# The second MLP product of a hybrid decoder step in wider matmuls, with 64 tokens as the stationary side

## The chip, the core and the metric

The kernel runs on one core of a Trainium2 chip. The metric is the time of one execution on the device, in microseconds (us). Five engines work side by side, each through its own queue of instructions in a fixed order: TensorE (PE, matmuls, with its weight loads in rows of their own, PEld), VectorE (DVE), ScalarE (ACT), GpSimd (POOL) and SyncE (SP), whose queue issues the DMA transfers. They wait for each other by semaphores.

## The reference

One step of one decoder layer for 288 tokens: 256 of a prompt, then 8 x 4 of samples. All is float32.

```python
h2 = rmsnorm(x, norm2_g)
f = jnp.square(jax.nn.relu(jnp.einsum("btd,df->btf", h2, w_ff1)))
x = x + jnp.einsum("btf,fd->btd", f, w_ff2)
```

D is 2048 and the MLP's inner width F is 8192. Before the MLP stand an input projection (2048 x 3072), a causal convolution of 31 taps, windowed means with small products, a LayerNorm and an output projection (2048 x 2048); behind it a last RMSNorm. The states of convolution and pooling are outputs too. The change is about the third line, `f` times `w_ff2`.

## The kernel before

Activations lie channel-major: 128 channels on the partitions, 288 tokens along the row. Every float32 operand of a large product is split exactly into two float32r parts, hi and lo, and a product is three: hi weight by hi activation, hi by lo, and lo by hi, summed in float32 in PSUM. In `gemm` (L223 to L236) that is three matmuls per tile of 128 x 128 weights, on lines L233, L234 and L235, each with the weights as the stationary side and 288 token columns moving.

Weights come in blocks of 1 MB, 1024 rows by 2 x 128 columns, by one DMA each (`load`, L142 to L151, queue SP), into `wr`, three buffers. `split` (L202 to L220) makes the hi part on ScalarE (L213, a cast) and the lo part on VectorE (L214, raw minus hi; in the first third also on GpSimd), 1024 columns an instruction, into four buffers each of `whi` and `wlo`. `weight_groups` is a generator of such splits in the order of use, and each `gemm` asks it for the next group at its end (`ready`), so that one group's weights are split while the group before is multiplied.

The MLP runs in four chunks of 2048 of the inner width (`FCH`), L440 to L475. In a chunk the first product makes 16 tiles of `f`, two at a time: eight `gemm` of 16 k tiles into two PSUM banks, then relu times the norm's factor (L452, DVE), the square and its hi part (L454, L456, ACT) and the lo part (L457, DVE). The second product then has eight groups of 256 output columns, each 16 k tiles by two banks by three matmuls, 96 in all, and adds the two banks to the residual `xT` (L466, DVE). Accumulators come from the pool `acc`, four banks, two for each group: the next group begins in two banks while DVE reads the other two. In the last chunk the squares for the last norm are taken on the way (L472, ACT; L474, DVE) and `xT` is scaled (L475, ACT); in the very last group one bank is finished ahead of the other (`m_outer`). `rsqrt_rows` (L177 to L197) then sums over the partitions with matmuls of one column (L182), goes through a chain of small operations, spreads the result (L196), and L481 multiplies and stores the output in six pieces.

Nobody writes the order on each engine out by hand: a scheduler with a timeline of its own orders the instructions by priority and estimated readiness, and places the waits. Thus a change of one part can shift the order of others.

Of the kernel before, what the change touches and what calls it, by code (L numbers as in the profile page):

```python
# [9 lines left out]
F32 = mybir.dt.float32  # L10
F32R = mybir.dt.float32r
# [5 lines left out]
P = 128  # L17
# [4 lines left out]
TB = T // 3  # L22
DC = DP = 1024
# [17 lines left out]
# groups of two 128-column results of the input projection, in order: a convolution tile's pair  # L41
# (a_i, gate_i), or a pooling group, the widest windows first
# [29 lines left out]
# per-channel vectors, [P, columns]: channel = column * P + partition  # L72
# [10 lines left out]
def trunk_kernel(ctx: ExitStack, tc: tile.TileContext, io):  # L83
    """Activations are channel-major: [channel on the partitions, token]. Tokens: the prompt's
    256, then 8 x 4 of the samples. Every float32 operand of a large product is split exactly in
    two float32r parts (12 bits each): w x = wh xh + wh xl + wl xh, in float32 accumulation."""
# [6 lines left out]
    actp = ctx.enter_context(tc.tile_pool(name="actp", bufs=40))  # L93
    tmpp = ctx.enter_context(tc.tile_pool(name="tmpp", bufs=8))
    prdp = ctx.enter_context(tc.tile_pool(name="prdp", bufs=2))
    acc = ctx.enter_context(tc.tile_pool(name="acc", bufs=4, space=PSUM))
    cvp = ctx.enter_context(tc.tile_pool(name="cvp", bufs=2, space=PSUM))
    msp = ctx.enter_context(tc.tile_pool(name="msp", bufs=2, space=PSUM))

# [16 lines left out]
    def act(name, **kw):  # L116
        return actp.tile([P, T], F32R, name=nm(name), **(kw or {"tag": "act"}))
# [7 lines left out]
    def f32(t):  # L125
        return t[:].bitcast(F32)
# [5 lines left out]
    vec = const.tile([P, NV], F32, name="vec")  # L132
    xT = const.tile([P, KT, T], F32, name="xT")
    u_all = const.tile([P, N8, UL], F32, name="u_all")
    z_all = const.tile([P, N8, ZL], F32, name="z_all")
# [6 lines left out]
    def load(cuts=((0, 8),), x_cuts=()):  # L142
        """The next 1 MB of weights; at the start in pieces, with pieces of x between them"""
# [18 lines left out]
    def load_table(func, src):  # L162
        """The function's table is loaded once src is there."""
# [6 lines left out]
    ident = const.tile([TB, TB], F32, name="ident")  # L170
# [6 lines left out]
    def rsqrt_rows(parts, scale, after=None):  # L177
        """PSUM [P, T], on every partition: 1 / sqrt(scale * sum over parts and partitions + eps)."""
# [14 lines left out]
        for j in range(3):  # L193
            nc.vector.tensor_scalar(dg[:TB, j * TB : (j + 1) * TB], ident, s[2][:, j : j + 1], None, op0=ALU.mult)
# [5 lines left out]
    turn = {"n": 0}  # L200

    def split(raw, share=0, cut=4):  # L202
        """[P, 8, 256] -> get(k, m): the parts of 128 columns; `share` of 8 on GpSimd"""
# [38 lines left out]
    hx = []  # L242
    for k in range(KT):
        hh, hl = act("hh"), act("hl")
# [6 lines left out]
    def weight_groups():  # L251
        """Per group of products, get(k, m) for each block of 8 k, in the order of the products."""
# [11 lines left out]
        for _ in range(2 * DFF // 256):  # L264
            yield [split(load()) for _ in range(2)]
# [23 lines left out]
    cs = []  # L289
    sum_c = row("sum_c")  # L290

    def conv_pair(i):
# [16 lines left out]
        c = actp.tile([P, T], F32, name=nm("c"), tag="c", bufs=8)  # L309
# [20 lines left out]
    dd = {}  # L330

    def pool_group(g):
# [3 lines left out]
        for m in range(2):  # L336
# [3 lines left out]
            tz = tmp("tz", T, "tz", 2)  # L340
# [4 lines left out]
            while w < WINDOWS[g]:  # L345
                s2 = tmp("s", ZL, "s", 4)
# [13 lines left out]
            dh, dl = act("dh", tag="p", bufs=16), act("dl", tag="p", bufs=16)  # L360
# [11 lines left out]
    mixp = {}  # L372
    for g in GROUPS:
        bk = bank2()
        gemm(bk, [dd[2 * g], dd[2 * g + 1]])
        for m in range(2):
            i = 2 * g + m
            mh, ml = act("ph"), act("pl")
# [21 lines left out]
    for i in range(N8):  # L400
        n = tmp("n")
        nc.vector.tensor_tensor(n, cs[i], rl[:, :T], op=ALU.mult)
        mh, ml = act("mh"), act("ml")
# [14 lines left out]
    x1 = []  # L418
    ss2 = row("ss2")
    for g in range(8):  # L420
        bk = bank2()
        gemm(bk, mixc)
        for m in range(2):
# [3 lines left out]
            kw = {"tag": "p", "bufs": 16} if k < 8 else {"tag": "c", "bufs": 8} if k >= 12 else {}  # L427
            ah, al = act("ah", **kw), act("al", **kw)
# [12 lines left out]
    r2 = row("r2")  # L441
    ssf = row("ssf")
    for ch in range(DFF // FCH):
        fx = []
        for g in range(FCH // 256):
# [4 lines left out]
            for m in range(2):  # L450
# [4 lines left out]
                fh, fl = act("fh"), act("fl")  # L455
# [85 lines left out]
```

## Time and profile before

| | |
|---|---|
| time, median of 3 runs (lowest to highest) | 1127.89 us (1125.96 to 1129.59) |
| the profiled execution, span from first to last instruction | 1125.9 us |
| PE busy | 1094.4 us, 97% |
| DVE, ACT, POOL busy | 677.1, 468.7, 188.8 us |
| mean granted TensorE clock | 0.987 |
| read from HBM | 181.49 MB, 165 GB/s over the span |
| a chunk's second product, PE | some 101 us, 768 matmuls |

No time is listed for the profiled execution beside its span; the lowest of the runs, 1125.96 us, equals the span, so that nothing that could be measured lies around it.

How to read the lines. A group of instructions reads: source line, engine, operation, tile written <- tiles read, shapes, count | busy us, mean ns of one | idle time of the engine just before, and what ended it. Names of buffers stand without their numbers: `ac` is a PSUM bank, `fh` and `fl` are the two parts of an `f` tile, `ah` and `al` those of the MLP's input, `ph` and `pl` those of the pooling half. The record of a matmul lasts longer than its slot, since matmuls are pipelined: what one costs is the distance from its start to the start of the next. A row of waits reads: who, at which line <- for whom: us in total, how often, the longest. A row of the timeline begins with its start and duration in us. A row of windows reads: from:to, length, then busy us and instructions of PE, PEld, DVE, ACT and POOL, the granted clock (1.00 is full), the share of the DMA engines and GB/s.

### The profile page before, as it was taken

How to read it: one execution, taken by the hardware profiler on the slowest of the kernel's cores; microseconds unless marked ns; L12 is line 12 of the kernel's file. 1: busy time of each engine (PE TensorE's matmuls, PEld its weight loads, DVE VectorE, ACT ScalarE, POOL GpSimd, SP SyncE). 2: the span in 40 equal slices, each digit the busy share in tenths (PEclk: the TensorE clock that was granted, in tenths of full speed). 3: DMA queues.
4: the chain of work that ended last, by engine and by line, in shares of the span. 5: the costliest groups of instructions: out<-in, count | busy, mean ns of one | idle time of the engine just before them, and what ended most of it. 6: DMA issues, size and time to landing. Idle time of an engine off the chain costs nothing.

```text
span 1125.9 us, 19336 instructions
## 1 busy us (share of the span) xinstructions
PE 1094.4 (97%) x8190; PEld 1089.8 (97%) x8190; DVE 677.1 (60%) x983; ACT 468.7 (42%) x643; POOL 188.8 (17%) x149
## 2 busy tenths in 40 slices
PE   7998898999999999999999999999999999999995
PEld 7998898999999999999999999999999999999995
DVE  7999999788755544445555444455444445555554
ACT  6443345356544433334444333344433334444441
POOL 4789886612200000000000000000000000000000
PEclk9999998989999999999999999999999999999998
DMA  8554438534445444444445454444444454545432
GB/s 298 191 175 164 148 115 222 184 113 166 172 150 177 160 171 167 158 179 154 184 153 183 152 182 156 174 163 167 170 160 178 153 184 151 183 155 175 162 113 84
DMA packets 31910, 187.01 MB, mean 166 GB/s; under 512 B 3408, under 2 KB 7760, under 8 KB 10448
## 3 DMA queue, kind: packets, MB, share of 16 engines
q1 hardware_dynamic: 31824, 185.78, 47.0%
q8 instruction: 64, 1.05, 0.4%
q14 instruction: 22, 0.18, 0.0%
HBM read 181.49 MB, written 4.28 MB: 165 GB/s over the span
## 4 chain that ended last, share of the span: by engine, by line
PE 86%; DVE 9%; POOL 2%; issue 2%; DMA 1%; ACT 0%; SPq 0%; DVEq 0%; POOLq 0%
PE ac L233 29%; PE ac L234 28%; PE ac L235 28%; DVE pc L316 3%; DVE wlo L214 1%; POOL wlo L214 1%; DVE d L354 1%; DVE ssc L397 1%; DVE d L351 1%; DMA xT<-in_xT 1%; POOL s L347 0%; DVE d L359 0%; DVE z_all L283 0%; PE pt L182 0%; DVE xT L481 0%
## 5 line engine op out<-in xcount | busy, mean ns | idle before, releaser
L213 ACT CAST whi<-wr 128x1024 fp32r<-128x1024 f32 (+1 forms) x342 | 355.0, 1040 | 562.8 <-PE ac L234 543.6
L214 DVE TENSOR_TENSOR wlo<-wr,whi 128x1024 fp32r<-128x1024 f32 (+1 forms) x295 | 364.7, 1236 | 371.8 <-ACT whi L213 371.7
L233 PE MATMUL ac<-ah,whi 128*128 128x288 f32 x1024 | 302.7, 296 | 0.0
L233 PE MATMUL ac<-fh,whi 128*128 128x288 f32 x1024 | 302.4, 295 | 0.0
L234 PE MATMUL ac<-al,whi 128*128 128x288 f32 x1024 | 301.2, 294 | 0.0
L234 PE MATMUL ac<-fl,whi 128*128 128x288 f32 x1024 | 301.2, 294 | 0.0
L235 PE MATMUL ac<-fh,wlo 128*128 128x288 f32 x1024 | 299.3, 292 | 0.0
L235 PE MATMUL ac<-ah,wlo 128*128 128x288 f32 x1024 | 298.8, 292 | 0.0
L235 PEld LDWEIGHTS ac<-fh,wlo 128*128 128x128 f32 x1024 | 193.1, 189 | 0.0
L235 PEld LDWEIGHTS ac<-ah,wlo 128*128 128x128 f32 x1024 | 192.9, 188 | 0.0
L234 PEld LDWEIGHTS ac<-fl,whi 128*128 128x128 f32 x1024 | 192.7, 188 | 0.0
L234 PEld LDWEIGHTS ac<-al,whi 128*128 128x128 f32 x1024 | 192.4, 188 | 0.1
L233 PEld LDWEIGHTS ac<-ah,whi 128*128 128x128 f32 x1024 | 192.1, 188 | 0.1
L233 PEld LDWEIGHTS ac<-fh,whi 128*128 128x128 f32 x1024 | 192.0, 188 | 0.0
L233 PE MATMUL ac<-hh,whi 128*128 128x288 f32 x384 | 113.6, 301 | 7.7 <-DVE tg L302 6.6
L214 POOL TENSOR_TENSOR wlo<-wr,whi 128x1024 fp32r<-128x1024 f32 (+1 forms) x47 | 112.3, 2400 | 34.0 <-ACT whi L213 31.4
L234 PE MATMUL ac<-hl,whi 128*128 128x288 f32 x384 | 114.9, 301 | 3.0 <-DVE hl L246 2.9
L235 PE MATMUL ac<-hh,wlo 128*128 128x288 f32 x384 | 114.2, 301 | 1.5 <-DVE wlo L214 1.4
L316 DVE SCALAR_TENSOR_TENSOR pc<-u_all,vec,pc 128x256 f32<-128x256 f32 x232 | 100.1, 479 | 1.3
L233 PEld LDWEIGHTS ac<-hh,whi 128*128 128x128 f32 x384 | 73.3, 193 | 8.4 <-issue 7.0
L234 PEld LDWEIGHTS ac<-hl,whi 128*128 128x128 f32 x384 | 74.3, 194 | 4.1 <-DVE hl L246 4.1
L235 PEld LDWEIGHTS ac<-hh,wlo 128*128 128x128 f32 x384 | 74.1, 194 | 2.3 <-DVE wlo L214 2.2
(115 smaller groups left out, 875.5 us busy)
## 6 DMA issues: line engine op xcount, KB each, us to landing
wr<-in_w SPq DMA_DIRECT2D x167, 1024.0 KB, 4.9
xT<-in_xT SPq DMA_DIRECT2D x8, 288.0 KB, 5.7
wr<-in_w SPq DMA_DIRECT2D x8, 256.0 KB, 5.6
out_u_out<-u_all SPq DMA_DIRECT2D x1, 1208.0 KB, 8.6
out_yT<-xT SPq DMA_DIRECT2D x2, 576.0 KB, 2.9
u_all<-in_hist_c SPq DMA_DIRECT2D x8, 136.0 KB, 5.8
out_z_out<-z_all SPq DMA_DIRECT2D x1, 668.0 KB, 7.4
z_all<-in_hist_p SPq DMA_DIRECT2D x4, 152.0 KB, 4.0
```

The costliest lines, as they stand in the source:

```text
L213: nc.scalar.copy(hi[:, k : k + cut, :], src)
L214: eng.tensor_tensor(lo[:, k : k + cut, :], src, hi[:, k : k + cut, :].bitcast(F32), op=ALU.subtract)
L233: nc.tensor.matmul(b, wh, xh, start=k == 0, stop=False)
L234: nc.tensor.matmul(b, wh, xl, start=False, stop=False)
L235: nc.tensor.matmul(b, wl, xh, start=False, stop=k == n - 1)
L316: nc.vector.scalar_tensor_tensor(out=dst, in0=up[:, w : w + SEQ], scalar=cwv[:, w : w + 1], in1=pc, op0=ALU.mult, op1=ALU.add)
L351: nc.vector.scalar_tensor_tensor(out=d[:, w - 1 : SEQ], in0=s[:, PH + w - 1 : ZO], scalar=1.0 / w, in1=z[:, PH + w - 1 : ZO], op0=ALU.mult ...
L354: nc.vector.scalar_tensor_tensor(out=samples(d[:, SEQ:T], NS), in0=ss[:, :, PH:], scalar=1.0 / w, in1=zs[:, :, PH:], op0=ALU.mult, op1=ALU ...
L397: nc.vector.tensor_tensor(ssc, ssc, q, op=ALU.add)
```

## The change

The second product is written anew; the first keeps its form. The tokens are divided: `TM` = 224, the main ones, and `TA` = 64, the tail. A tile of `f` now lies in one row of 576 columns: lo of the main tokens (224), hi of all (288), lo of the tail (64). So 448 adjoining columns are lo and hi of the main tokens, the 288 in the middle are hi of all, and the last 128 are hi and lo of the tail. VectorE writes the lo part in two pieces.

Output columns are taken 512 at a time, in four groups a chunk, and a group is four calls of `gemm4`, each over four k tiles (a quarter of the chunk's width). For each k tile a call issues:

- one matmul with the tail's 128 columns (hi and lo of 64 tokens) as the stationary side and 512 columns of hi weights moving, into the bank `tok`: token-major partial results, hi by hi in the upper 64 partitions, hi by lo in the lower;
- for each of four tiles of 128 output columns, one matmul of hi weights by the 448 columns, into columns 0 to 447 of that tile's bank, and one of lo weights by the 288 columns, into columns 224 to 511. So a bank holds the main tokens in two pieces that are still to be added, and the lo-weight part of the tail behind them.

All four banks of `acc` thus belong to one group, and `tok` takes a bank of the pool that the convolution used (`cvp`, two banks). `split4` splits half the rows of two blocks at once, into `vhi` and `vlo`, two buffers each of 4 x 512 columns, and the blocks of `w_ff2` come in pairs of adjoining columns. At a group's end `tok` is copied (first chunk, ACT) or added (DVE) to `y_tok` [128, 2048], and each bank is added to `xT` in two operations, of 224 and of 288 columns. In the last chunk each group's part of `y_tok` is transposed by PE against the identity (`tp`), and DVE adds its two halves to the tail's columns of `xT` before the banks' second pieces. `m_outer` is not used by the new form.

To make room, tiles that only the first part needs (`u_all`, `z_all`, `prd`, and the temporaries `tz` and `s`) are in a pool `earp` that is closed before the MLP; `latep`, which holds `y_tok`, `vhi` and `vlo`, comes in its place. Pairs of hi and lo activations are now one tile of two rows (`act`), half as many buffers of twice the size, and the convolution's results lie in pairs (`cp`).

```diff
-        for c in range(0, D, 256):
+        for c in range(0, D, 512):
             for r in range(ch, ch + FCH, 1024):
-                yield "w_ff2", r, (c, c + P)
+                for cc in (c, c + 256):
+                    yield "w_ff2", r, (cc, cc + P)
...
+    def split4(raws, h):
+        hi = late_pool[0].tile([P, 4, 512], F32R, name=nm("vhi"), tag="vhi", bufs=2)
+        lo = late_pool[0].tile([P, 4, 512], F32R, name=nm("vlo"), tag="vlo", bufs=2)
+        for j, raw in enumerate(raws):
+            src = raw[:, 4 * h : 4 * h + 4, :]
+            cols = slice(256 * j, 256 * j + 256)
+            nc.scalar.copy(hi[:, :, cols], src)
+            nc.vector.tensor_tensor(lo[:, :, cols], src, hi[:, :, cols].bitcast(F32), op=ALU.subtract)
+        return hi, lo
+
+    def gemm4(banks, tokens, rhs, first, last):
+        hi, lo = ready.pop()
+        for k, x in enumerate(rhs):
+            nc.tensor.matmul(tokens, x[:, TM + T - TA : 2 * T], hi[:, k, :], start=first and k == 0, stop=last and k == 3)
+        for m, b in enumerate(banks):
+            for k, x in enumerate(rhs):
+                cols = slice(m * P, (m + 1) * P)
+                nc.tensor.matmul(b[:, 0 : 2 * TM], hi[:, k, cols], x[:, 0 : 2 * TM], start=first and k == 0, stop=False, skip_group_check=True)
+                nc.tensor.matmul(b[:, TM:512], lo[:, k, cols], x[:, TM:512], start=False, stop=last and k == 3, skip_group_check=True)
+        ready.extend(itertools.islice(weights, 1))
...
+            for _ in range(D // 512 * FCH // 1024):
+                raws = [load(), load()]
+                for h in range(2):
+                    yield split4(raws, h)
...
-                nc.vector.tensor_tensor(fl, f, f32(fh), op=ALU.subtract)
+                nc.vector.tensor_tensor(x[:, 0:TM], f[:, 0:TM], f32(fh[:, 0:TM]), op=ALU.subtract)
+                nc.vector.tensor_tensor(x[:, TM + T :], f[:, TM:T], f32(fh[:, TM:T]), op=ALU.subtract)
...
-        for g in range(8):
-            bk = bank2()
-            gemm(bk, fx, m_outer=last and g == 7)
-            for m in range(2):
-                k = 2 * g + m
+        for g in range(D // 512):
+            tok = cvp.tile([P, 512], F32, name=nm("tok"), tag="cv")
+            bk = bank2() + bank2()
+            for j in range(FCH // 512):
+                gemm4(bk, tok, fx[4 * j : 4 * j + 4], j == 0, j == FCH // 512 - 1)
+            yt = y_tok[:, g * 512 : (g + 1) * 512]
+            if ch == 0:
+                nc.scalar.copy(yt, tok)
+            else:
+                nc.vector.tensor_tensor(yt, yt, tok, op=ALU.add)
+            if last:
+                tp = ms("tp")
+                for m in range(4):
+                    nc.tensor.transpose(tp[:, m * P : (m + 1) * P], yt[:, m * P : (m + 1) * P], ident)
+                xa = xT[:, 4 * g : 4 * g + 4, TM:T]
+                for h in range(2):
+                    nc.vector.tensor_tensor(xa, xa, tp[:].rearrange("p (m t) -> p m t", t=P)[:, :, h * TA : (h + 1) * TA], op=ALU.add)
+            for m in range(4):
+                k = 4 * g + m
                 xk = xT[:, k, :]
-                nc.vector.tensor_tensor(xk, xk, bk[m][:, :T], op=ALU.add)
+                nc.vector.tensor_tensor(xk[:, 0:TM], xk[:, 0:TM], bk[m][:, 0:TM], op=ALU.add)
+                nc.vector.tensor_tensor(xk, xk, bk[m][:, TM : TM + T], op=ALU.add)
```

More of the change, by code (lines that the diff above doesn't have):

```diff
@@ L22 @@
 TB = T // 3
+TA = 64
+TM = T - TA
 DC = DP = 1024
@@ L98, in trunk_kernel @@
     msp = ctx.enter_context(tc.tile_pool(name="msp", bufs=2, space=PSUM))
+    early = ExitStack()
+    earp = early.enter_context(tc.tile_pool(name="earp", bufs=1))
+    prdp = early.enter_context(tc.tile_pool(name="prdp", bufs=2))
     seen = {}
@@ L116, in act @@
     def act(name, **kw):
-        return actp.tile([P, T], F32R, name=nm(name), **(kw or {"tag": "act"}))
+        t = actp.tile([P, 2, T], F32R, name=nm(name), **(kw or {"tag": "act"}))
+        return t[:, 0, :], t[:, 1, :]
     def tmp(name, n=T, tag="tmp", bufs=6):
@@ L263, in weight_groups @@
             yield [split(load())]
-        for _ in range(2 * DFF // 256):
-            yield [split(load()) for _ in range(2)]
+        for _ in range(DFF // FCH):
+            for _ in range(FCH // 256):
+                yield [split(load()) for _ in range(2)]
+            for _ in range(D // 512 * FCH // 1024):
+                raws = [load(), load()]
+                for h in range(2):
+                    yield split4(raws, h)
     weights = weight_groups()
@@ L289, in trunk_kernel @@
     cs = []
+    cp = [actp.tile([P, 2, T], F32, name=nm("c"), tag="c", bufs=4) for _ in range(N8 // 2)]
     sum_c = row("sum_c")
@@ L438, in trunk_kernel @@
                     nc.gpsimd.tensor_tensor(ss2, ss2, q2, op=ALU.add)
+    early.close()
+    latep = ctx.enter_context(tc.tile_pool(name="latep", bufs=1, reuse_waits="tile"))
+    late_pool.append(latep)
     r2 = row("r2")
     ssf = row("ssf")
+    y_tok = latep.tile([P, D], F32, name="y_tok")
     for ch in range(DFF // FCH):
```

37 lines of the change are left out of this document (19 added, 18 removed).

## The prediction, made before the changed kernel had run

> **What bounds the kernel now.** I read the page's shares first, then the waits of the MLP, then its groups and the timeline.
>
> ```profile
> PE 1094.4 (97%) x8190; PEld 1089.8 (97%) x8190; DVE 677.1 (60%) x983; ACT 468.7 (42%) x643; POOL 188.8 (17%) x149
> PE 86%; DVE 9%; POOL 2%; issue 2%; DMA 1%; ACT 0%; SPq 0%; DVEq 0%; POOLq 0%
> ```
>
> TensorE holds 86% of the chain that ended last. The waits between 330 and 1111 us, where the MLP runs, have no row in which PE waits:
>
> ```profile
> ACT whi L213 <- PE ac L234: 463.5, 244, 2.1
> DVE wlo L214 <- ACT whi L213: 355.6, 245, 2.0
> DVE xT L466 <- PE ac L235: 21.5, 32, 3.2
> SPq L150 <- DVE wlo L214: 708.7, 120, 5.9
> ```
>
> Everybody waits for the matmuls, and the weight loads wait for a raw buffer. So the second product costs what its matmuls cost, and a change of it pays or loses on PE's pitch and wherever it gives PE a wait. The windows of two second products, the last and the one before it, and the ends of the last:
>
> ```profile
> 808.20:909.50 101.30, 101.30 (x770) 101.30 (x769) 46.72 (x51) 34.95 (x36) 0.00 (x0) 1.00 0.47 166
> 1010.40:1111.40 101.00, 101.00 (x771) 101.00 (x770) 49.23 (x62) 43.47 (x63) 0.00 (x0) 1.00 0.36 126
> L233 PE MATMUL ac<-fh,whi 128*128 128x288 f32 x1024 | 302.4, 295 | 0.0
> L234 PE MATMUL ac<-fl,whi 128*128 128x288 f32 x1024 | 301.2, 294 | 0.0
> L235 PE MATMUL ac<-fh,wlo 128*128 128x288 f32 x1024 | 299.3, 292 | 0.0
> 1010.51 0.29 PE L233 MATMUL ac<-fh,whi 128*128 128x288 f32 x1
> 1111.29 0.29 PE L235 MATMUL ac<-fh,wlo 128*128 128x288 f32 x1
> ```
>
> Three lines with 1024 matmuls each over four chunks make 768 per chunk: 100.78 us over 767 steps is a pitch of 131.4 ns. What would the columns alone take? At half clock the same matmul shows it:
>
> ```profile
> 239.00:242.00 3.00, 3.00 (x14) 3.00 (x14) 1.34 (x2) 1.24 (x2) 0.00 (x0) 0.50 0.70 292
> 239.17 0.44 PE L234 MATMUL ac<-pl,whi 128*128 128x288 f32 x1
> 239.41 0.44 PE L235 MATMUL ac<-ph,wlo 128*128 128x288 f32 x1
> ```
>
> 240 ns per 288 columns at a granted 0.50; halved, 120 ns, 0.4167 ns a column. So 11.4 ns of each pitch at full clock is not columns, if all of the 240 is. (With one and the same toll in both it would be 2 x 131.4 - 240 = 22.8 ns.) Only this part can the change win.
>
> **The change, part by part.**
>
> *Columns and instructions.* Per k tile and 512 weight columns the old form has 4 x 3 matmuls of 288 columns, 3456 columns. The new one has one of 512 (token stationary), four of 448 and four of 288: again 3456. No column is saved; nine matmuls stand where twelve stood, 256 times over (64 k tiles, four groups of 512).
>
> What becomes of the 11.4 ns is the unknown. If it is a toll per matmul, three tolls go: 256 x 3 x 11.4 ns = 8.7 us gained. If it is a rate (288 columns in 131.4 ns, the operands not coming faster), 512 + 4 x 448 columns cost eight old matmuls, and the gain is 0. The third reading comes from the nearest longer matmul, the float32 one of the mean:
>
> ```profile
> 222.26 0.65 PE L385 MATMUL pmean<-sum_c,ones 128*128 128x288 f32 x2
> 222.53 0.51 PE L235 MATMUL ac<-ph,wlo 128*128 128x288 f32 x1
> 222.88 0.29 PE L233 MATMUL ac<-ph,whi 128*128 128x288 f32 x1
> ```
>
> 222.26 to 222.88 less one pitch of 0.131 leaves 489 ns for two passes, 244.5 each. If each streams 240 ns, only 4.4 ns is toll: a longer pass hides it. Then wide ones cost 191.1 and 217.7 ns, the 288s stay at 131.4: 1507.7 instead of 1576.8 ns, 256 x 69.1 = 17.7 us gained (the toll of 22.8 would make 17.5). Against that stands the load alone:
>
> ```profile
> 314.59 0.25 PEld L182 LDWEIGHTS pt<-ones,ss 128*96 128x96 f32 x2
> 314.76 0.25 PEld L182 LDWEIGHTS pt<-ones,q 128*96 128x96 f32 x2
> 315.27 0.19 PEld L233 LDWEIGHTS ac<-ah,whi 128*128 128x128 f32 x1
> 315.38 0.19 PEld L234 LDWEIGHTS ac<-al,whi 128*128 128x128 f32 x1
> ```
>
> One load of 96 columns every 85 ns, one of 128 in 110: less than 120, so the load is hidden already at 288 columns and should not be what makes 131.4. I take the toll, 8.7 us, between the ends 0 and 17.7. A quarter (four k tiles) is then 6.17 us: tokens 0.90, each bank 1.32.
>
> The Trainium skill, "TensorE: Matmul & The Clock Gate", section "Back-to-back issue gap", gives columns/2.4 + 2.5 ns at full clock. For 288 that is 122.5, and the trace has 131.4: they differ. Taken for the wide matmuls alone it makes 189.2 and 215.8 ns and a gain of 20.1 us, so it speaks for the third reading.
>
> *Waits added.* Durations that the boundaries need:
>
> ```profile
> L214 DVE TENSOR_TENSOR wlo<-wr,whi 128x1024 fp32r<-128x1024 f32 x289 | 359.3, 1243 | 371.1 <-ACT whi L213 371.1
> L466 DVE TENSOR_TENSOR xT<-xT,ac 128x288 f32<-128x288 f32 x64 | 27.2, 454 | 26.4 <-PE ac L235 26.4
> L481 DVE TENSOR_TENSOR xT<-xT,pr 128x1152 f32<-128x1152 f32 x2 | 2.6, 1348 | 0.0
> L481 DVE TENSOR_TENSOR xT<-xT,pr 128x576 f32<-128x576 f32 x2 | 1.5, 746 | 0.0
> L213 ACT CAST whi<-wr 128x1024 fp32r<-128x1024 f32 x334 | 350.1, 1050 | 561.8 <-PE ac L234 543.6 <-issue 8.1 <-ACT ah L429 4.1
> L472 ACT ACTIVATE q<-xT 128x288 f32<-128x288 f32 x15 | 5.9, 434 | 9.6 <-DVE xT L466 9.6
> L475 ACT ACTIVATE xT<-xT,vec 128x288 f32<-128x288 f32 x16 | 7.7, 524 | 0.1
> DMA to landing us min/median/max: 4.5/4.9/11.1
> 1111.42 0.25 PE L182 MATMUL pt<-ones,ssf 128*96 128x1 f32 x2
> 1111.62 0.46 DVE L466 TENSOR_TENSOR xT<-xT,ac 128x288 f32<-128x288 f32 x1 [4.88 <-PE ac L235]
> 1112.60 0.33 PE L182 MATMUL pt<-ones,q 128*96 128x1 f32 x2 [0.93 <-ACT q L472]
> ```
>
> The L481 rows give 1.04 ns a column: an add of 224 columns 0.39, of 256 0.42, of 512 0.69 us. DVE sees PE's end 0.2 us late (last matmul over at 1111.42, add at 1111.62). All four accumulators now belong to one group; before, two of four were free at each change. Times below run from the start of a group's last quarter, PE's end 6.17; DVE works in the order in which the changed program issues.
>
> Between groups in chunks 1 to 3: token add 1.10-1.79, two lo splits to 4.27, then two adds of 224 and two of 288. Bank 0 is free at about 5.5 and wanted at 6.17 + 0.90: no wait. The splits' second block is loaded only when a buffer is read out 3.7 us before this quarter; 4.9 later it lands at 1.2, its copy ends at 2.3, in time. Cost 0, with 1.5 us to spare; without that cover each us of lateness costs a us.
>
> Between chunks 2 and 3, and 3 and 4, the first product starts with no token matmuls ahead, and DVE has split (3.55), token add (4.25), split (5.5), 224, 224 (6.3), 288 (6.73) before bank 0 is free: 0.6 us each, 1.2 in all. After chunk 1 ScalarE copies the tokens, and the wait is gone.
>
> In the last chunk PE transposes the tokens at each group's end: four float32 matmuls, two passes of 128 columns each at the load's 110 ns, 0.9 us, to 7.05. DVE then has two adds of 256 (to 8.1), a lo split (9.3) and the 288 add that frees bank 0 at 9.8. PE fills in with the tokens of the next two quarters (the second from 8.5, when ScalarE's two copies after 6.37 are done, to 9.4): 1.0 us idle. 1.9 us for each of three changes, 5.7.
>
> The tail: from 7.05 + 0.2 two adds of 256 and four of 288 end at 9.9. ScalarE takes squares and scales in turn (434 and 524 ns) and ends the last square at 11.4, 5.3 us after PE's last product matmul; before it was 1111.42 to 1112.60, 1.2. Cost 4.1. What follows is the same.
>
> *Hidden edits.* The lo activation written in two pieces and the split adds cost a fixed 0.155 us a piece (454 ns less 288 x 1.04), 0.3 us per 256 columns of the first product, on a DVE that is 49% busy in the last window above; nothing on the path unless DVE fills up. Loads: the same megabytes in another order, one per 6.17 instead of 6.3 us, at a DMA share of 0.47. Pooled early tiles reshuffle the instructions of the first 300 us; from nothing in the trace can I tell the sign, and take 0 within 2 us.
>
> Sum: -8.7 + 1.2 + 5.7 + 4.1 = +2.3 us. The profiled execution spans 1125.9 us, as the fastest run (1125.96); the median of the three runs is 2.0 above. 1127.9 + 2.3 = 1130.2 us.
>
> **The rivals.**
> *Wide matmuls hide the toll* (other side, faster): 17.7 instead of 8.7 gained, 1121.2 us; by the skill's formula 1118.8. For it the mean's 4.4 ns, against it the load's 110 ns. It decides from a pitch of the 448s under about 194 ns.
> *A rate, no gain* (the change does not do what it says): 448 columns cost 204 ns, 1138.9 us. For it: no toll shows at half clock or in the half-rate float32 pass, as a limit on columns per ns would have it.
> *The pairs starve* (slower): a block's load can start only when the pair before is split, three buffers serve pairs of two, and copies need all 512 columns before the first token matmul. Landing later by the 1.5 us to spare costs; with 1 us on each of 32 pairs, 1162 us. Against it the median of 4.9; for it the maximum of 11.1. A lost clock belongs here too:
>
> ```profile
> 235.32 0.33 PE L182 MATMUL pt<-ones,ssc 128*96 128x1 f32 x2 [2.04 <-DVE ssc L397]
> ```
>
> PE idled 2.04 us there, and the half clock of the window from 239 follows. The last chunk's stalls could do the same: three times 3 us at half clock lose (240 - 131) / 240 each, 4 us in all, 1134.
>
> **How the numbers follow.** Toll per matmul 0.45 (1130; alone 1125 to 1136), rate 0.20, wide hides 0.22, starving or clock 0.13. About 0.3%, 3.4 us, can be told from no change, so 1124.5 to 1131.3 is the same. Faster 0.25: the hiding case nearly whole, and the low edge of the first. Same 0.26: half of the first. Slower 0.49: its upper part and the two others. The range 1119 to 1142 leaves out the worst stalls and the best hiding.
>
> **What would show it.** Pitch: the 448s start-to-next 198 ns (hides 191, rate 204), the 512s 225 (218, 234). Waits of PE: for the DVE add before bank 0 in three places of the last chunk, about 1 us each, and little elsewhere; the chain's end with a square 5.3 us after the last product matmul. Wrong I would be by PE rows that wait for a hi copy or a load throughout the MLP, by a granted clock under 1.00 there, or by a first product that starts some us off the 301.62 of this row:
>
> ```profile
> 301.62 0.30 PE L233 MATMUL ac<-ah,whi 128*128 128x288 f32 x1
> ```

## The result, and the profile after

The changed kernel takes 1136.16 us (median of four runs, 1135.38 to 1137.22); the kernel before, on the same chip, 1126.93 us (1125.07 to 1129.59). The ratio is 1.0084, with a 95% interval from 1.0067 to 1.0101: some 9.5 us slower. 1130.2 us was predicted, in a range of 1119 to 1142; the sign was the likeliest one, the size was 6 us short (7 in the change, since a fourth run has moved the median before from 1127.89 to 1126.93). The profiled execution took 1136.49 us with a span of 1134.7, against a span of 1125.9 before: 8.8 us to be explained. Each run of the changed kernel takes 1.7 to 1.8 us more than its span. So 1125.9 will be the span of a run of some 1127.7 us, an estimate, and that the fastest run equals it does not show that nothing lies around the span, as the section on the time before has it; the forecast, added to the median, does not depend on this.

From the page of the changed kernel, the shares of the engines and the chain that ended last:

```profile
PE 1096.3 (97%) x7438; PEld 1064.0 (94%) x7438; DVE 700.9 (62%) x1131; ACT 464.9 (41%) x647; POOL 187.2 (16%) x149
PE 87%; DVE 10%; ACT 1%; issue 1%; DMA 0%; SPq 0%; DVEq 0%; POOL 0%; POOLq 0%; ACTq 0%
```

TensorE is still what counts. With 752 matmuls fewer PE is busy 1.9 us longer in all, so even there next to nothing was gained. Its waits from 300 to 1136 us, in the changed kernel:

```profile
PE pt L190 <- DVE ssf L536: 4.1, 1, 4.1
PE pr L204 <- DVE dg L202: 2.0, 1, 2.0
PE tok L249 <- ACT vhi L239: 1.7, 3, 0.6
```

The first and the last row are new; both lie in the last chunk and behind it. To see where the 8.8 us are, cut both traces at the starts of the MLP's stretches. Windows of the changed kernel: first product of chunk 2, second product of chunk 2, first product of chunk 4, second product of chunk 4 up to its last product matmul's end, the wait behind it, the norm's small matmuls, and the output:

```profile
505.21:606.78 101.57, 101.57 (x770) 101.57 (x769) 52.16 (x78) 42.73 (x60) 0.00 (x0) 1.00 0.50 175
606.78:707.06 100.28, 100.28 (x579) 93.90 (x577) 51.95 (x71) 33.67 (x36) 0.00 (x0) 1.00 0.43 158
909.02:1010.67 101.65, 101.65 (x769) 101.65 (x769) 52.82 (x80) 42.51 (x60) 0.00 (x0) 1.00 0.50 176
1010.67:1115.13 104.46, 102.71 (x591) 94.76 (x589) 53.91 (x82) 39.36 (x56) 0.00 (x0) 1.00 0.31 111
1115.13:1119.86 4.73, 0.60 (x7) 0.39 (x5) 4.06 (x10) 2.70 (x8) 0.00 (x0) 0.87 0.00 0
1119.86:1125.20 5.34, 3.32 (x14) 2.46 (x14) 1.43 (x8) 0.68 (x3) 0.00 (x0) 0.50 0.00 0
1125.20:1134.70 9.50, 0.02 (x1) 0.00 (x0) 5.28 (x6) 0.00 (x0) 0.00 (x0) 0.50 0.63 248
```

The same stretches of the kernel before (first product of chunk 2, second product of chunk 2, second product of chunk 4, the norm, the output):

```profile
505.55:606.46 100.91, 100.91 (x771) 100.91 (x769) 51.24 (x63) 42.94 (x60) 0.00 (x0) 1.00 0.47 167
606.46:707.37 100.91, 100.91 (x771) 100.91 (x770) 46.75 (x51) 34.94 (x36) 0.00 (x0) 1.00 0.47 167
1010.51:1111.42 100.91, 100.91 (x770) 100.91 (x769) 49.12 (x62) 43.47 (x63) 0.00 (x0) 1.00 0.36 126
1111.42:1116.29 4.87, 2.01 (x16) 1.38 (x14) 1.88 (x9) 1.18 (x3) 0.00 (x0) 0.99 0.00 0
1116.29:1125.90 9.61, 0.00 (x0) 0.00 (x0) 5.28 (x6) 0.00 (x0) 0.00 (x0) 0.50 0.62 246
```

All stretches, from one start to the next, in us (the middle ones read from the trace in the same way):

| stretch | before | after | difference |
|---|---|---|---|
| up to the MLP's first matmul | 301.62 | 301.80 | +0.2 |
| first products, chunks 1 to 4 | 102.60, 100.91, 100.91, 100.91 | 103.14, 101.57, 101.54, 101.65 | +2.6 |
| second products, chunks 1 to 3 | 101.33, 100.91, 101.33 | 100.27, 100.27, 100.42 | -2.6 |
| second product, chunk 4, to the last product matmul's end | 100.91 | 104.46 | +3.5 |
| from there to the end | 14.48 | 19.57 | +5.1 |

So the rewritten stretches of chunks 1 to 3 gain 2.6 us, the first products, whose code is the same but for the storage of hi and lo, lose it again, and the last chunk and its tail make the result.

Why so little is gained: the beginning of a second product in the changed kernel (timeline: start, length, instruction).

```profile
606.78 1.09 PE L249 MATMUL tok<-vhi,fx 128*128 128x512 f32 x4
607.71 0.37 PE L253 MATMUL ac<-fx,vhi 128*128 128x448 f32 x1
...
612.72 0.36 PE L253 MATMUL ac<-fx,vhi 128*128 128x448 f32 x1
612.92 0.29 PE L254 MATMUL ac<-fx,vlo 128*128 128x288 f32 x1
613.06 1.09 PE L249 MATMUL tok<-vhi,fx 128*128 128x512 f32 x4
```

607.71 less 606.78 is 0.93 us for four token matmuls, 232 ns each (225 predicted). From 607.71 to 613.06 stand 16 pairs of a 448 and a 288, 334 ns a pair, of which the 448 has some 201 (198 predicted) and the 288 some 133 (131.4). Over the 16 quarters of the chunk a quarter is 100.27 / 16 = 6.267 us; predicted were 6.17, and four k tiles of the old form at 131.4 ns took 100.91 / 16 = 6.307. Over 64 quarters that is 2.6 us gained of 8.7. (That the table has 2.6 for three chunks as well is chance: there 0.8 comes from the two stretches of 101.33.)

The change of group in the last chunk, and the tail, in the changed kernel's timeline:

```profile
1035.76 0.60 PE L520 MATMUL tp<-ident,y_tok 128*128 128x128 f32 x4
1036.11 1.18 PE L249 MATMUL tok<-vhi,fx 128*128 128x512 f32 x4
1037.87 1.20 PE L249 MATMUL tok<-vhi,fx 128*128 128x512 f32 x4 [0.58 <-ACT vhi L239]
1038.91 0.44 PE L253 MATMUL ac<-fx,vhi 128*128 128x448 f32 x1
...
1115.00 0.29 PE L254 MATMUL ac<-fx,vlo 128*128 128x288 f32 x1
1115.13 0.60 PE L520 MATMUL tp<-ident,y_tok 128*128 128x128 f32 x4
1115.33 0.39 DVE L527 TENSOR_TENSOR xT<-xT,ac 128x224 f32<-128x224 f32 x1 [0.95 <-PE ac L254]
1115.77 0.88 DVE L523 TENSOR_TENSOR xT<-xT,tp 128x256 f32<-128x256 f32 x2
1116.67 1.54 DVE L528 TENSOR_TENSOR xT<-xT,ac 128x288 f32<-128x288 f32 x4
1119.86 0.45 PE L190 MATMUL pt<-ones,ssf 128*96 128x1 f32 x2 [4.13 <-DVE ssf L536]
1120.17 0.46 PE L190 MATMUL pt<-ones,q 128*96 128x1 f32 x2
```

The four transposes take 0.35 us, the tokens of two quarters stand in a row because the banks are not free yet, and the second of them waits for ScalarE's copy. At the end DVE adds the transposed halves and four second pieces in a chain; the column sums of the square follow 5.0 us after the last product matmul's end (1115.13 to 1120.17), where it was 1.2. In that pause the granted clock falls to 0.50, as the windows show, and from these column sums to the end it is 14.5 us (1120.17 to 1134.7) where it was 13.3 (1112.60 to 1125.9).

### The profile page after: what moved, and what is told of

Same layout as the page of the kernel before. It is cut to its first block, busy times and chain, and to the rows that moved or that the text cites. A ratio compares the mean times of both kernels' runs of the same rounds, so it can differ in the third digit from the quotient of the medians.

```text
span 1134.7 us, 17926 instructions
## 1 busy us (share of the span) xinstructions
PE 1096.3 (97%) x7438; PEld 1064.0 (94%) x7438; DVE 700.9 (62%) x1131; ACT 464.9 (41%) x647; POOL 187.2 (16%) x149
## 4 chain that ended last, share of the span: by engine, by line
PE 87%; DVE 10%; ACT 1%; issue 1%; DMA 0%; SPq 0%; DVEq 0%; POOL 0%; POOLq 0%; ACTq 0%
PE ac L253 18%; PE ac L267 17%; PE ac L269 17%; PE ac L268 17%; PE ac L254 12%; PE tok L249 5%; DVE pc L356 3%; DVE d L394 1%; DVE wlo L223 1%; DVE ssc L437 1%; DVE hx L280 1%; ACT vhi L239 1%; DVE d L391 1%; DMA xT<-in_xT 0%; PE pt L190 0%
## 5 line engine op out<-in xcount | busy, mean ns | idle before, releaser
L253 PE MATMUL ac<-fx,vhi 128*128 128x448 f32 x1024 | 343.1, 363 | 0.0
L223 DVE TENSOR_TENSOR wlo<-wr,whi 128x1024 fp32r<-128x1024 f32 (+1 forms) x167 | 204.6, 1227 | 176.5 <-ACT whi L222 176.5
L267 PE MATMUL ac<-ax,whi 128*128 128x288 f32 x1024 | 302.6, 296 | 0.0
L268 PE MATMUL ac<-ax,whi 128*128 128x288 f32 x1024 | 301.1, 294 | 0.0
L269 PE MATMUL ac<-ax,wlo 128*128 128x288 f32 x1024 | 300.7, 294 | 0.0
L254 PE MATMUL ac<-fx,vlo 128*128 128x288 f32 x1024 | 299.4, 294 | 0.0
L253 PEld LDWEIGHTS ac<-fx,vhi 128*128 128x128 f32 x1024 | 191.9, 188 | 16.7 <-issue 0.8
L254 PEld LDWEIGHTS ac<-fx,vlo 128*128 128x128 f32 x1024 | 192.3, 188 | 2.5
L268 PEld LDWEIGHTS ac<-ax,whi 128*128 128x128 f32 x1024 | 193.5, 189 | 0.1
L269 PEld LDWEIGHTS ac<-ax,wlo 128*128 128x128 f32 x1024 | 193.3, 189 | 0.0
L267 PEld LDWEIGHTS ac<-ax,whi 128*128 128x128 f32 x1024 | 191.8, 187 | 0.3 <-PE ac L253 0.3
L267 PE MATMUL ac<-hx,whi 128*128 128x288 f32 x384 | 116.2, 304 | 8.5 <-DVE tg L342 6.6
L268 PE MATMUL ac<-hx,whi 128*128 128x288 f32 x384 | 115.6, 302 | 0.2
```

The lines of the kernel that those rows point to most:

```text
L223: eng.tensor_tensor(lo[:, k : k + cut, :], src, hi[:, k : k + cut, :].bitcast(F32), op=ALU.subtract)
L253: nc.tensor.matmul(b[:, 0 : 2 * TM], hi[:, k, cols], x[:, 0 : 2 * TM], start=first and k == 0, stop=False, skip_group_check=True)
L254: nc.tensor.matmul(b[:, TM:512], lo[:, k, cols], x[:, TM:512], start=False, stop=last and k == 3, skip_group_check=True)
L267: nc.tensor.matmul(b, wh, xh, start=k == 0, stop=False)
L268: nc.tensor.matmul(b, wh, xl, start=False, stop=False)
L269: nc.tensor.matmul(b, wl, xh, start=False, stop=k == n - 1)
```

## The experiments

All but e10 were run once, so each is read from the stretches of its trace, not from its time. Theory after the result: a matmul in float32r pays a toll, but wide ones pay more of it than 288 columns do; the first products are slowed by the places of hi and lo in one tile; and the last chunk pays for the transposes' adds on DVE. Rivals: a rate in columns per ns, a load of weights that is not hidden, a wait in the first products, a falling clock.

**e1: the pitch by width.** The changed kernel with blocks of 40 matmuls appended behind its end, each with other weights than the one before:

```diff
+        for name, n in (("ra", 64), ("rb", 128), ("rc", 192), ("rd", 256), ("re", 288), ("rf", 352), ("rg", 448), ("rh", 512)):
+            block(name, (n,))
+        block("oa", (288,), off=16)
+        block("ob", (448,), off=64)
+        block("la", (288,), m=64)
+        block("lb", (288,), m=32)
+        block("lc", (448,), m=64)
+        block("pp", (448, 288))
+        for name, n in (("ba", 128), ("bb", 288), ("bc", 448), ("bd", 512)):
+            block(name, (n,), s=sb, x=mb)
```

> The changed kernel, with blocks of 40 matmuls behind its last store that nothing reads (time as a whole is longer and says nothing): float32r, weights changing with each matmul, 64, 128, 192, 256, 288, 352, 448 and 512 columns, then 288 and 448 columns from other offsets, then stationary sides of 64 and 32 columns, a block that alternates 448 and 288, and bfloat16 with 128, 288, 448 and 512. Toll per matmul: the pitch is columns/2.4 + 11 to 13 ns from 256 columns up (448: 199, 512: 226), whatever the stationary side. Rate: the part over columns/2.4 grows with the columns, 11.4 ns at 288, 17.7 at 448, 20.3 at 512. Contention with the weight load: the part over columns/2.4 falls to a half or less with 64 stationary columns and to a quarter with 32 (288: 126 and 123). Wide matmuls hide it: 448 at 191, 512 at 218. If it is the 4-byte operands, bfloat16 shows 2 to 5 ns in place of 11.

Its timeline (one row is a whole block; `lc` has 64 columns of weights, `bc` and `bd` are bfloat16):

```profile
1165.56 5.43 PE L495 MATMUL re<-mv,stw 128*128 128x288 f32 x40
1170.83 6.56 PE L495 MATMUL rf<-mv,stw 128*128 128x352 f32 x40
1177.23 8.27 PE L495 MATMUL rg<-mv,stw 128*128 128x448 f32 x40
1185.33 9.25 PE L495 MATMUL rh<-mv,stw 128*128 128x512 f32 x40
1218.25 8.26 PE L495 MATMUL lc<-mv,stw 128*64 128x448 f32 x40
1240.24 7.73 PE L495 MATMUL bc<-mb,sb 128*128 128x448 bf16 x40
1247.81 8.80 PE L495 MATMUL bd<-mb,sb 128*128 128x512 bf16 x40
```

A block's length less one matmul's own record, by 39, is its pitch: 8.27 less 0.365 gives 202.7 ns for `rg`. All of them, from the starts at full clock, in ns:

| columns | 64, 192 | 256 | 288 | 352 | 448 | 512 |
|---|---|---|---|---|---|---|
| float32r | 112 | 120.4 | 131.8 | 160.0 | 202.7 | 227.3 |
| above columns x 0.4167 | | 13.7 | 11.8 | 13.3 | 16.0 | 14.0 |
| bfloat16 | | | 122.5 | | 189.2 | 215.8 |

The block of 128 columns, and that of 192 but for its last 15 steps, ran at half clock, at 213 ns a matmul. The excess is about the same for 256 and for 512 columns, so it is no rate; it does not vanish in wide matmuls, so nothing is hidden. With 64 columns of weights instead of 128 the 448 takes 202.4 and the 288 takes 130.1, so it isn't the weight load either. But the 448s and 512s pay 2 to 4 ns more than the 288s, and that eats more than half of what three tolls fewer bring. In bfloat16 the same widths pay 2.5 ns: most of the toll goes with float32r. (Alternating 448 and 288 takes 339 ns a pair here, 334 in the kernel's own stream.) The Trainium skill, "TensorE: Matmul & The Clock Gate", section "Back-to-back issue gap", gives columns/2.4 + 2.5 ns at full clock for what it calls the isolated gap; by it 288, 448 and 512 columns take 122.5, 189.2 and 215.8 ns. The bfloat16 blocks agree to 0.1 ns; the float32r ones, which this kernel uses, are 9 to 14 ns above it.

**e2: the kernel before with paired tiles.** Only the storage of the changed kernel, not its matmuls:

```diff
-    actp = ctx.enter_context(tc.tile_pool(name="actp", bufs=40))
+    actp = ctx.enter_context(tc.tile_pool(name="actp", bufs=20))
...
-        return actp.tile([P, T], F32R, name=nm(name), **(kw or {"tag": "act"}))
+        t = actp.tile([P, 2, T], F32R, name=nm(name), **(kw or {"tag": "act"}))
+        return t[:, 0, :], t[:, 1, :]
```

> The kernel before, with hi and lo activations as two rows of one tile (half as many buffers of twice the size) and nothing else of the change. In the changed kernel the first product's chunks take 101.55 to 101.65 us, before 100.91. Theory that the paired tiles' places cost it: chunks of the first product at 101.5 here, the whole 2 to 3 us over the kernel before (1129 to 1130). Rival, that the pools moved by the early and late pool do: 100.9 here, 1127.

Measured: 1135.82 us beside 1125.95 for the kernel before. From the second on, all stretches of the MLP have one length (the second product of chunk 2):

```profile
611.03:712.58 101.55, 101.55 (x770) 101.55 (x769) 46.80 (x51) 34.93 (x36) 0.00 (x0) 1.00 0.48 166
```

101.55 / 768 is 132.2 ns, where the kernel before has 131.4: 4.2 us over the eight stretches. Most of the rest of the 7.8 us between the spans (1133.7 and 1125.9) is that the MLP begins at 304.80 us instead of 301.62, as the scheduler has ordered the first part anew. So the loss in the first products comes without any of the new matmuls. That it is the tiles' places, as I then thought, had to be tried.

**e5: same and separate tiles, started differently.** Behind the changed kernel, blocks of 96 matmuls in the first product's order, with hi and lo as rows of one tile (`qs`), swapped (`qb`), in two tiles (`qa`), or mixed (`qm`), each three times behind other matmuls:

```diff
+        for name, first in (("1", ()), ("2", (352,)), ("3", (64, 448, 320))):
+            block("qs" + name, same, first)
+            block("qb" + name, back, first)
+            block("qa" + name, apart, first)
+            block("qm" + name, mixed, first)
```

> The changed kernel with blocks of 96 matmuls of the first product's form (288 columns; wh xh, wh xl, wl xh in turn, two banks) appended behind its end, so the whole takes some 180 us longer. qs: hi and lo are two rows of one tile; qb: the same with lo in the lower row; qa: hi and lo from two tiles; qm: these three mixed; each of them three times, behind nothing, behind one matmul of 352 columns, behind matmuls of 64, 448 and 320 columns. If the places of hi and lo set the pitch: qs1, qs2 and qs3 alike near 132.2 ns, qa1, qa2 and qa3 alike near 131.4. If the pitch is a beat that a stretch falls into by the moment at which it starts: the numbers 1, 2 and 3 of one letter differ, or all letters agree, between 129.9 and 132.3.

Measured, in ns, from the first of a block's 288-column matmuls to its last: `qs` 132.2, 132.5, 132.2; `qb` 132.2, 131.2, 132.1; `qa` 132.5, 132.5, 132.2; `qm` 132.6, 131.9, 132.3. A last block that reads one row of one tile throughout, `qo`, has 131.6. Two tiles are no faster than one, and the same tiles (`qb`) are at 132.2 or at 131.2 with another matmul ahead. Its timeline, the first two blocks of `qb`:

```profile
1158.19 0.30 PE L503 MATMUL qb<-mv,wp 128*128 128x288 f32 x1
...
1170.88 0.29 PE L503 MATMUL qa<-mv,wp 128*128 128x288 f32 x1
...
1209.38 0.30 PE L503 MATMUL qb<-mv,wp 128*128 128x288 f32 x1
...
1221.96 0.32 PE L497 MATMUL qa<-mv,wp 128*128 128x352 f32 x1
```

12.69 us for 96 in the first, 12.58 in the second. So one tile for hi and lo does not by itself give the higher pitch, nor do two tiles give the lower. In the traces a stream repeats a short pattern of slots, a beat: nine matmuls of some 1180 ns together (131.1 each) or twelve of 1587 (132.2). The changed kernel's first products keep the second of them. The 131.4 of the kernel before is a mix of both, and its groups of 96 change over at one and the same matmul each time. A group of the second product of chunk 2 there:

```profile
606.46 0.29 PE L233 MATMUL ac<-fh,whi 128*128 128x288 f32 x1
...
609.63 0.29 PE L233 MATMUL ac<-fh,whi 128*128 128x288 f32 x1
...
619.07 0.29 PE L233 MATMUL ac<-fh,whi 128*128 128x288 f32 x1
```

The first 24 matmuls take 3.17 us, 132.2 ns each, the other 72 take 9.44 us, 131.1 each. In chunk 4 it is the same but for the last group; in the second products of chunks 1 and 3, the ones of 101.33 us, the last 60 of each group are at 132.2; in the first products the first 72 are at 131.1 and the last 24 at 132.2.

**e6: hi and lo apart again in the changed kernel.** Two hi parts now share a tile, and two lo parts another.

```diff
-            ah, al = act("ax", **kw)
+            if m == 0:
+                his, los = act("axh", **kw), act("axl", **kw)
+            ah, al = his[m], los[m]
```

> The changed kernel, but the first product's activations lie two hi parts to a tile and two lo parts to a tile, so that hi and lo of one k tile are in different tiles as before the change. If hi and lo in one tile are what slowed the first products: chunks 2 to 4 take about 100.9 us each instead of 101.55 and the span falls by 2.6 us, apart from the first 302 us, which may shift by up to 3.5 us as the planner reshuffles them. If it is not the tiles: 101.5 stays, or another of the levels 100.9, 101.3 and 101.55 comes up.

Measured: 1138.6 us; the first products of chunks 2 to 4 take 101.99 us each, 132.8 ns a matmul, a further level and worse than before. Putting the tiles apart in this way is no remedy.

**e8 and e9: the beat in the kernels themselves.** One extra matmul ahead of each group of 96:

```diff
+        c = 208 + 8 * (3 * nudges["n"] % 10)
+        nc.tensor.matmul(ms("nd")[:, 0:c], x[:, 0:P], x[:, 0:c], start=True, stop=True)
...
+            nudge(x1[0][0])
             gemm(bk, x1)
```

> The kernel before, with one matmul of 208 to 280 columns (ten widths in turn, result unused) ahead of each of the MLP's 64 groups of 96 matmuls of 288 columns, so that each group starts at another moment; some 0.12 us each, 8 us in all. If the pitch is a beat that a stretch falls into by how it starts: the 64 groups' pitches spread over several levels between 131.1 and 132.8 ns, 131.39 no longer the rule. If something fixed in this program sets it (tiles, addresses): 131.39 stays in nearly all groups.

> The changed kernel with the same nudges ahead of the 32 groups of its first products. If a beat: spread over the same levels as the kernel before, nudged, with a like mean. If something fixed in this program: 132.22 stays in nearly all groups.

In the kernel before, nudged, 22 of the 61 groups that the trace shows in full settle at 131.2 to 131.5 ns (over their last 65 steps) and 39 at 132.1 to 132.7. Two groups of the first product of chunk 1, behind nudges of 272 and of 216 columns, each from its first matmul to the next nudge:

```profile
363.80 0.29 PE L233 MATMUL ac<-ah,whi 128*128 128x288 f32 x1
...
376.42 0.26 PE L243 MATMUL nd<-ah 128*128 128x216 f32 x1
376.52 0.30 PE L233 MATMUL ac<-ah,whi 128*128 128x288 f32 x1
...
389.25 0.28 PE L243 MATMUL nd<-ah 128*128 128x240 f32 x1
```

12.62 us and 12.73 us for 96 matmuls of the same lines on the same activations, both at full clock. In the first products the level goes with the nudge: of the 27 full groups that are not the first of their chunk, the nine behind 208, 272 or 280 columns take 131.4 to 131.5 ns a matmul, the 18 behind the other widths 132.3 to 132.6. So how a group starts has a part in it. But it is not all. In the second products the last 60 matmuls of a group run at 132.2 ns in all 16 groups of chunks 1 and 3, and at 131.1 in 12 of the 15 full groups of chunks 2 and 4, almost whatever the nudge, the levels that they have without nudges. There something that stays with the chunk decides; where the tiles of `f` lie is a candidate that no run isolates. e9 says less: the scheduler moved the nudges of chunks 2 to 4 into the second products, and only chunk 1 was nudged; its five full groups are at 132.1 to 132.4.

So the 2.6 us that the first products lost came with the storage in pairs: e2 has the 132.2 with nothing else of the change, and so have all kernels here with the changed kernel's own tiles. That pairs must cost it is not shown (`qb` reached 131.2), and what decides the beat stays open.

**e3 and e4: the last chunk.** e3 adds the banks to `xT` ahead of the transposed halves; e4 leaves transposes and their adds out, so the last 64 tokens lack that part of the second product.

```diff
             for m in range(4):
+                xk = xT[:, 4 * g + m, :]
                 nc.vector.tensor_tensor(xk[:, 0:TM], xk[:, 0:TM], bk[m][:, 0:TM], op=ALU.add)
                 nc.vector.tensor_tensor(xk, xk, bk[m][:, TM : TM + T], op=ALU.add)
+            if last:
+                xa = xT[:, 4 * g : 4 * g + 4, TM:T]
+                for h in range(2):
+                    nc.vector.tensor_tensor(xa, xa, tp[:].rearrange("p (m t) -> p m t", t=P)[:, :, h * TA : (h + 1) * TA], op=ALU.add)
```

> The changed kernel with the last chunk's adds in another order: each group's banks are added to the residual first, the transposed tail after them. Theory that the banks are held by the transposed adds: the second token matmul's wait of 0.75 us stays (it waits for a hi copy), the first bank's waits go; the last chunk's second product falls from 109.2 by 1 to 3 us, the time to 1133 to 1135. Rival, that the transposes on PE and the hi copies are all that it costs: no change within 0.5 us in the stretch between two groups.

> The changed kernel without the last chunk's transposes and the add of the tail's tokens into the residual: the last 64 tokens lack the part of the second product that is kept token-major. Theory that the last chunk's excess of 8.9 us over the other chunks' second products is the transposes with what they hold up, in three changes of group and at the end: here the last chunk's changes of group cost nothing and the end some 2.5 us less, the time 1128 to 1130. Rival, that the end (one bank not finished ahead of the others, squares in a row) costs most: 1132 to 1134.

e3, a change of group in its timeline:

```profile
1031.96 0.60 PE L520 MATMUL tp<-ident,y_tok 128*128 128x128 f32 x4
1032.31 1.17 PE L249 MATMUL tok<-vhi,fx 128*128 128x512 f32 x4
1033.32 0.37 PE L253 MATMUL ac<-fx,vhi 128*128 128x448 f32 x1
```

The tokens of one quarter alone stand there, nothing waits, and a change costs 0.45 us: the transposes' 0.35 and 0.1 more in the first token matmul. In the changed kernel it costs (104.46 - 100.27) / 3 = 1.40 us. The order of the adds made 0.95 us of each. The wait for the hi copy, which was expected to stay, went too. With the wait behind it the last second product takes 106.05 us instead of 109.19, within what was expected. The tail stays: PE waits 3.7 us instead of 4.1. (Of e3's time, 1129.47 us, 3.5 us less are due to the first part, which ends at 298.29 us in this program; that is not the edit's merit.) The same stretch in e4:

```profile
1010.09:1111.85 101.76, 100.42 (x578) 93.74 (x577) 54.26 (x84) 42.89 (x63) 0.00 (x0) 1.00 0.31 114
```

It takes 101.76 us instead of 109.19, and the span is 1125.8: without transposes and their adds the loss is gone, though the first products still have their 132.2 ns.

**e7 and e10: the transposes moved.** Ahead of the last bank of a group, with the fourth bank's adds last; in e7 as products with a stacked identity and one add, in e10 as the changed kernel's transposes and two adds.

```diff
         for m, b in enumerate(banks):
+            if between is not None and m == len(banks) - 1:
+                between()
...
+                if last and m == 3:
+                    xa = xT[:, 4 * g : 4 * g + 4, TM:T]
+                    for h in range(2):
+                        nc.vector.tensor_tensor(xa, xa, tp[:].rearrange("p (m t) -> p m t", t=P)[:, :, h * TA : (h + 1) * TA], op=ALU.add)
```

> The changed kernel, with the last chunk's transposes ahead of the last bank of a group's last quarter, done as products with a stacked identity of 64 columns (which adds the hi and lo halves), one add in place of two, and the fourth bank's adds last. If the 8.3 us that the last second product costs more are the transposes on PE (16 of 0.22 us = 3.5) plus waits and a long tail on VectorE: the last second product takes about 104 us instead of 109.2, with no wait of the bank or token matmuls over 0.3 us at its three changes of group and about 1.5 us from PE's last product matmul to the square's column sums. If it is the clock or the scheduling of weights in the last chunk: 107 us or more stay.

> As e7, but with the changed kernel's own transposes (one pass of 109 ns each by its trace, where the stacked products took two of 112) and its two adds. Expected from the changed kernel's rows: last second product 100.3 + 4 groups of 0.5 + 1.9 for the tail = 104.2 us, against 109.2 in the changed kernel and 105.7 with stacked products; without the first 302 us some 827 us against 832.9 and 824.3 before, so about 3 us slower than the kernel before (0.2 to 0.4%), with up to 3 us either way from the reshuffled first part. If the two adds in place of one hold VectorE up at the end: the tail takes 2.5 us or more and e7 stays the better one.

e7, 1132.88 us: the last second product and the wait take 105.73 us, not 104, since four products with 64 columns are two passes each, 0.87 us a group, where four transposes take 0.35. e10: 104.65 us (104.2 expected); its windows, to the last product's end, the wait, the norm:

```profile
1013.63:1115.82 102.19, 102.19 (x594) 95.48 (x592) 56.17 (x87) 39.17 (x56) 0.00 (x0) 1.00 0.31 114
1115.82:1118.28 2.46, 0.00 (x1) 0.00 (x1) 2.16 (x6) 2.31 (x7) 0.00 (x0) 1.00 0.00 0
1118.28:1122.78 4.50, 2.48 (x14) 1.59 (x14) 1.42 (x8) 1.03 (x3) 0.00 (x0) 0.64 0.00 0
```

The clock no longer drops ahead of the column sums, and from the MLP's first matmul to the end it takes 1132.3 - 304.77 = 827.5 us, against 832.9 in the changed kernel and 824.3 before. 5.4 of the 8.6 us are recovered. Its time is 1133.55 us (1130.36 to 1134.48, four runs), since its first part happens to end at 304.77 us; the ratio to the kernel before is 1.0064 (1.0046 to 1.0082). No version here beats the kernel before: four second products gain 2.6 us on the 100.91 us of the shorter old ones, four sets of transposes cost 1.8, and the tail about 2.

## Why the prediction came out as it did

*The matmuls: -8.7 predicted, -2.6 measured.* The step that failed is the size of the toll in wide matmuls. A constant toll was the right kind (e1: no rate, no hiding, not the load), but the 11.4 ns of the 288s were carried over to widths that the trace did not have. The 448s pay 14.5 ns and the 512s 19, the 288s among them 12.8: nine matmuls pay 4 x (14.5 + 12.8) + 19 = 128 ns where twelve paid 137, and 9 x 11.4 = 103 had been reckoned. The bounds, 0 and 17.7, held it; I took the value nearest to the row that I had, and the float32 pass that spoke for hiding was no guide to float32r.

*First products: nothing predicted, +2.6 measured.* Paired tiles were costed only for the first 300 us. The 131.4 ns that I took for a property of 288 columns was a mix of two beats, 131.1 and 132.2; with hi and lo in pairs, all 96 of a group are at 132.2 (e2), by a mechanism that stays open. The trace of before had held a hint: its second products took 101.33 us in chunks 1 and 3 and 100.91 in 2 and 4, in the same code.

*Changes of chunk: 1.2 predicted, about 0.3 measured.* The first products of chunks 3 and 4 begin 0.0 to 0.1 us late, beyond 768 matmuls of 132.22 ns, and the second product of chunk 3 has 0.15 us more than its neighbours. DVE was in time for bank 0.

*Changes of group in the last chunk: 1.9 each predicted, 1.40 measured.* The place and the mechanism were right: transposes, then PE through two quarters' tokens until DVE has freed a bank. But a transpose is one pass of 109 ns, not two. Of the 1.0 us in which PE was to stand, some 0.55 was for ScalarE's second copy and the rest for DVE's add before bank 0, the wait named as the sign to look for. The first came, 0.6 us; of the second the profile has no row.

*The tail: 4.1 predicted, 5.1 measured.* The last square stands 5.0 us behind the last product matmul (5.3 predicted). What was missing is that this pause halves the clock for the norm's small matmuls behind it: 14.5 us instead of 13.3 to the end, 1.2 more, where the prediction had what follows as the same. The half clock had been named as a rival for stalls of 3 us between groups; there the longest wait was 0.6 us and the clock stayed at 1.00.

*Hidden edits and starving: nothing predicted, nothing found.* DVE is busy 51 to 52% of the windows of the MLP, and PE has no row of a wait for a load. The first part, within 2 us by the prediction, moved by 0.2; but e3, e2 and e10 have it at 298.3, 304.8 and 304.8 us, so 2 us was too narrow.

Sum, predicted and measured: matmuls -8.7 / -2.6, and -0.8 for the two slower stretches of before (0.42 each); first products 0 / +2.5 (2.6 less the 0.1 of late starts); changes of chunk +1.2 / +0.3; of group +5.7 / +4.2; tail +4.1 / +5.1; first part 0 / +0.2: +2.3 against +8.9, the 8.8 of the spans but for rounding. The sign was right because the costs of the last chunk, worked out from rows, were larger than the gain in any but the third reading; the point was low by what wide matmuls and the beat took. It came no further off by luck: 6.1 us too much on the matmuls, 2.5 us of the first products and 1.0 us of the tail were partly covered by changes of chunk and group that came 2.4 us cheaper, and by the 0.8 us of the old stretches.

## What to carry to other kernels

A pitch that one shape shows is no price for another shape: the part above the columns' time must be measured at the width that the change will use, and where a few ns decide, an unchanged stream must be expected to move by 1% when its tiles, or what runs ahead of it, change. A rewritten inner loop pays its gain per chunk, but a second layout has to be brought back at the end, where nothing covers it; price that end first, with what the pause does to the clock. When adds free accumulators, those that free a bank go ahead of those that merely finish a result: that order alone was worth 0.95 us at each of three changes.

## What the runs showed of the hardware that was not expected

- float32r matmuls of 64 and of 192 columns both take 112 ns at full clock; from 256 columns on they take columns x 0.4167 ns and 10 to 16 more, with 32, 64 or 128 columns of weights. In bfloat16 it is 2.5 more at 288, 448 and 512 columns (e1).
- A stream of 288-column float32r matmuls runs in one of a few repeating patterns of slots: 131.1 or 132.2 ns each in the kernels before and after, 132.8 in e6. It can change from one to the other at a fixed matmul of each group (after 24 of 96 in the second product of chunk 2 before), and an extra matmul ahead of a group can change it (e8). What else decides it is open.
- A float32 transpose of 128 columns is one pass of 109 ns; a float32 product with 64 columns is two passes of 112 ns (e7).
- A pause of 4.1 us on TensorE was followed by half the granted clock, and pairs of one-column matmuls came every 0.32 us. After one of 2.5 us (e10) they still came every 0.17 us, and the clock fell behind them.
- Forty matmuls of 64 columns back to back, 4.4 us at full clock, were followed by half the clock, though PE never paused; it lasted through the forty of 128 columns behind them (e1).
